# Softmax times V: the verdict is loaded in the last pass, and the first head's spread stands in the middle branch

## The chip, the cores and the metric

The kernel runs on one core of one Trainium2 chip. The metric is the device time of one execution in microseconds; the median of several runs is given. The core has five engines: TensorE (matmuls; "PE" and "PEld" in the profile, its sequencer "PEq"), VectorE ("DVE"), ScalarE ("ACT"), GpSimd ("POOL") and SyncE ("SP"), which here issues all transfers. Each engine runs its own instruction stream; they meet through semaphores.

## The reference

```python
# scores: (8, 12, 1024, 1024) float32, v: (8, 12, 1024, 64) float32, both drawn from a normal distribution
scores_max = np.max(scores, axis=-1, keepdims=True)
attn = np.exp(scores - scores_max)
attn = attn / (np.sum(attn, axis=-1, keepdims=True) + 1e-8)
return np.matmul(attn, v).astype(np.float32)
```

There are 96 heads. Scores are 403 MB, V and the output 25 MB each.

## The kernel before, in words

**Passes and heads.** A `For_i` loop makes `PASSES` = 24 passes, each over `AHEAD` = 4 heads. They are handled two at a time, so that a pass has `K` = 2 steps, k = 0 and k = 1 (the text calls such a step a head: the first head, the second head). A step has 128 partitions (64 for each of its two heads) and `R` = 16 rows of 1024 scores in each partition.

**A row.** ScalarE takes the exponential, two rows an instruction (L460; one row at a time for the last four of the second head); the maximum is not subtracted. TensorE transposes the result in eight 128 x 128 blocks into PSUM (L473), VectorE copies it to `pt` (L485, L481), and TensorE multiplies it with `vones`, V with a column of ones at its side (L172), so that the sum of the exponentials comes out as one more column. The products of a row follow its transposes by `LAG` = 3 rows: `finish` takes the oldest row from `pending`. TensorE's order is written out by hand (`in_line`).

**Normalisation.** Three rows share a PSUM bank (`psO`), so that 16 rows make six groups and the last group has one row. `normalise` takes the reciprocal of the sums into a column of `seen` (`invert`, L150), and then VectorE multiplies with it, once for each half of the partitions (L158), into `out_bufs`.

**V.** A pass's V is loaded as `v_sb` (`load_v`, L308). GpSimd spreads it into `vones` with eight casts for each head (`spread_v`, L320): for k = 0 behind the last products of the first head, for k = 1 at the pass's end. In the last pass there is no further V, but the spread for k = 0 is executed all the same. GpSimd also puts finished rows by in `done` (L202), which is stored in the next pass.

**Branches.** `load_first` stands behind the transposes of the first head's last row. If more passes follow, it loads V, stores the pass before and loads the next pass's first scores (a condition inside cuts the load in three for the last passes). Otherwise it stores what the two passes before left. `last` stands at the end of the pass: either spread, put by and load, or, in the last pass, `end` (three stores of the last rows, L237), `fold` and `judge`. All five engines execute every branch, also those in which they have nothing to do; an engine that has skipped instructions raises its semaphore by as many in the other arm (the balance).

**The verdict.** Sums of exponentials may overflow for other inputs, and V may be too large. `seen` keeps the reciprocals and the largest |V|; `fold` reduces them (L352, L353). `judge` makes one column `right` of two comparisons (L361, L364), TensorE counts it with a matmul against ones (L369), and VectorE writes the count (L373). Behind the loop each engine loads the count into a register (`nc.values_load`, L511) and branches (L515) over `general`, the slow kernel, which is not executed for these inputs.

**Order of transfers.** SP issues in program order; the names in `queued` chain the instructions. The loop does without a barrier between passes (`iteration_sync="reg_based"`): waits are on semaphore values that registers hold.

Of the kernel before, what the change touches and what calls it, by code (L numbers as in the profile page):

```python
# [9 lines left out]
FP16 = mybir.dt.float16  # L10
# [16 lines left out]
def kernel(  # L27
# [16 lines left out]
    G = 3  # L44
# [87 lines left out]
    def in_line(op):  # L132

        if line:
            after(op, line[-1])
        line.append(op)
# [16 lines left out]
    def normalise(k, st, g):  # L153
# [10 lines left out]
            fills.append(norm)  # L164
        norms[k] = norm

    def finish(u):

        _, k, r, pt, st = u
        g, i = r // G, r % G  # L170
        for c in range(C):
            product = nc.tensor.matmul(  # L172
                out=st["psO"][g][:, i * M : (i + 1) * M],
                lhsT=pt[:, c * P : (c + 1) * P],
                rhs=vones[:, k, c].rearrange("p t n -> p (t n)")[:, 0:M],
                start=(c == 0),
                stop=(c == C - 1),
            )
            in_line(product)
        if i == G - 1 or r == R - 1:  # L180
            normalise(k, st, g)
        if r == R - 1 and k < K - 1:
            fold()
            spread_v(k)

    def behind(a, b, reason):

# [63 lines left out]
    stores, fills, ends, norms = [], [], [], {}  # L251
    writers, users = {}, {}

    def apart(a, b, reason="stores of two heads are disjoint"):
# [19 lines left out]
    def load(k, m, parts=(R,), r=0, **cond):  # L274
        rows_n = sc_rows[bass.ds(m, 1), k].rearrange("o x r k -> (o x) r k")
        for rows in parts:
            queue(
                nc.sync.dma_start(  # L278
                    out=s_bufs[k][:, r : r + rows, :], in_=rows_n[:, r : r + rows, :], **cond
                )  # L280
            )
            r += rows

    def load_first(m):

# [30 lines left out]
    def spread_v(k, behind_rows=False):  # L316

        for t in range(T):
            for s in range(S):
                op = nc.gpsimd.tensor_copy(  # L320
                    out=vones[s * Q : (s + 1) * Q, k, :, t, 0:D].rearrange(
                        "i (h l) d -> i h l d", l=L
                    ),
                    in_=v_sb[(k * T + t) * Q : (k * T + t + 1) * Q, :, s],
                )
# [16 lines left out]
    def small(name, dtype=FP32):  # L342
        turn[name] = turn.get(name, 0) + 1
        return small_pool.tile([P, 1], dtype, name=f"{name}{turn[name]}")

    count = small_pool.tile([1, 1], I32, name="count")
    right = small("right", FP16)

    def fold():

        n = K * R + 1
        nc.vector.tensor_reduce(out=seen[:, 0:1], in_=seen[:, 0 : n + 1], axis=X, op=ALU.min)  # L352
        nc.vector.tensor_reduce(  # L353
            out=seen[:, n + 1 : n + 2], in_=seen[:, 1 : n + 2], axis=X, op=ALU.max
        )

    def judge(bank):

        n = K * R + 1
        part = small("part")  # L360
        nc.vector.tensor_scalar(  # L361
            out=part, in0=seen[:, n + 1 : n + 2], scalar1=1.0, scalar2=None, op0=ALU.is_le
        )
        nc.vector.scalar_tensor_tensor(  # L364
            out=right, in0=seen[:, 0:1], scalar=1.0 / SUM_MAX, in1=part, op0=ALU.is_ge, op1=ALU.mult
        )
        cell = bank[0:1, G * M : G * M + 1]
        in_line(
            nc.tensor.matmul(  # L369
                out=cell, lhsT=right[:], rhs=vones[:, 0, 0, 0, D : D + 1], start=True, stop=True  # L370
            )
        )
        nc.vector.tensor_copy(out=count[:], in_=cell)  # L373

    def general():

# [39 lines left out]
                out=o_rows[bass.ds(n, 1)].rearrange("o p d -> (o p) d"), in_=out_row  # L416
            )

    def last(m, bank):

        before = queued[-1:]
        k = K - 1
        with tc.If(m < PASSES - 1) as cmp:
            n = nc.snap(m + 1, min_val=1, max_val=PASSES - 1)
            with tc.If(m < PASSES - 2) as cmp3:
                behind(put_by(0), norms[0], "all rows are there")
                spread_v(k, True)
                watch_v()
                put_by(k)
            with cmp3.Else():  # L430
                spread = spread_v(k)
                watch = watch_v()
                gate = nc.gpsimd.tensor_copy(out=cell, in_=out_bufs[k][:, R - 1, D - 1 : D])
                for op in (watch, spread):
                    behind(gate, op, "the values have been read")
                put_spare()
            with tc.If(m < PASSES - 3) as cmp2:  # L437
# [12 lines left out]
    def heads(m):  # L450

        for k in range(K):
            st = dict(psO=[take(psO_bufs) for g in range(GROUPS)])
            for r in range(R):
# [29 lines left out]
                elif r % EB == EB - 1:  # L484
                    copy = nc.vector.tensor_copy(out=pt2[:], in_=psT2[:])  # L485
# [12 lines left out]

    assert BH % AHEAD == 0 and BH >= 3 * AHEAD and SK == Q * S * C and K == 2
    load_v(0)  # L500
# [5 lines left out]
    with tc.For_i(0, PASSES, 1, iteration_sync="reg_based") as m:  # L506
# [1 line left out]
        line.clear()  # L508
        heads(m)

    good = nc.values_load(  # L511
        count[:], min_val=0, max_val=P,
        skip_runtime_bounds_check_because="a count of partitions, which is compared and no address",
    )
    with tc.If(good < P, preferred_fallthrough_block=False):  # L515
        general()


# [28 lines left out]
```

## Time and profile before

| | |
|---|---|
| median of 3 runs | 1058.47 us (1058.43 to 1059.35) |
| the profiled execution | 1058.32 us, its span 1056.6 us |
| bytes moved | 453 MB, mean 429 GB/s |
| busy: TensorE, VectorE, ScalarE, GpSimd | 77%, 67%, 71%, 40% |

The page's times are microseconds from the start of the span. "L320" is line 320 of the kernel. In a line of the timeline stand the start, the length, the engine, the line and the operation, its output and input, the count, and in brackets how long the engine was idle before and what ended that. In an answer about one line stand the count, the shortest, median and longest duration in ns, and the first and last start. A window's line has its length, the busy time of TensorE, its weight loads, VectorE, ScalarE and GpSimd with their counts, then the granted TensorE clock, the transfer engines' share and GB/s.

### The profile page before, as it was taken

Reading aid. Unit: us, or ns where it says so; the run is one execution under the profiler, and the core shown is the slowest. Engines: PE = TensorE matmul, PEld = TensorE weight load, DVE = VectorE, ACT = ScalarE, POOL = GpSimd, SP = SyncE. Lnnn points to the kernel's source line nnn. Section 1 sums busy time; section 2 is a strip of 40 time slices with the busy share of each in tenths; the row PEclk is TensorE's granted clock in tenths of the full one; section 3 lists DMA queues with packets and bytes.
Section 4 is the critical chain, followed back from the end, with each engine's and each line's share of the span. In section 5 each row is a group of like instructions: output and inputs, shape, how many; then the busy total and the mean of one; then the engine's idle time right before and its main releaser. Section 6 shows DMA issues by size and latency. Waiting matters only on the chain.

```text
span 1056.6 us, 32648 instructions
## 1 busy us (share of the span) xinstructions
PE 812.9 (77%) x12289; PEld 777.5 (74%) x12289; DVE 705.7 (67%) x1352; ACT 750.2 (71%) x484; POOL 423.6 (40%) x579
## 2 busy tenths in 40 slices
PE   3488678787787868878678877787687876878887
PEld 3488668686787867878678777787677866868786
DVE  2377666676676756768567675676656766667787
ACT  4487578776787667876778667786687856877985
POOL 3063343533525335343362433633426334353341
PEclk9799889888898988889888898898988988989999
DMA  9999999999999999999999999999999999999997
GB/s 397 438 437 429 406 452 437 427 422 429 444 437 437 437 432 441 437 429 429 429 422 434 437 437 437 437 437 417 457 429 429 432 414 439 437 437 423 428 420 325
DMA packets 16692, 453.06 MB, mean 429 GB/s; under 512 B 1840, under 2 KB 1968, under 8 KB 2992
## 3 DMA queue, kind: packets, MB, share of 16 engines
q1 hardware_dynamic: 16688, 452.99, 99.6%
q8 instruction: 4, 0.07, 0.0%
HBM read 427.82 MB, written 27.26 MB: 431 GB/s over the span
## 4 chain that ended last, share of the span: by engine, by line
DMA 61%; PE 14%; ACT 10%; PEld 9%; DVE 3%; POOL 1%; issue 1%; SPq 0%; ACTq 0%; POOLq 0%; PEldq 0%; DVEq 0%
DMA s_nat<-in_scores_dram 61%; ACT p_nat L460 10%; PE psT L473 7%; PE psO L172 7%; PEld L172 4%; PEld L473 4%; DVE pt L485 3%; POOL vones L320 1%; POOL done L202 0%; SPq L278 0%; DVE out_sb L158 0%; DVE seen L150 0%; ACTq L460 0%; DVE pt L481 0%; SPq L308 0%
## 5 line engine op out<-in xcount | busy, mean ns | idle before, releaser
L460 ACT ACTIVATE p_nat<-s_nat 128x2048 f16<-128x2048 f32 (+1 forms) x432 | 702.5, 1709 | 284.2 <-SPq L437 157.9
L473 PE MATMUL psT<-ident,p_nat 128*128 128x128 f16 x6144 | 520.6, 235 | 212.7 <-ACT p_nat L460 212.5
L485 DVE COPY pt<-psT 128x2048 f16<-128x2048 f16 x336 | 411.3, 1224 | 307.2 <-PE L473 143.3
L473 PEld LDWEIGHTS <-p_nat 128*128 128x128 f16 x6144 | 435.6, 120 | 227.9 <-ACT p_nat L460 225.3
L172 PE MATMUL psO<-vones,pt 128*128 128x130 f16 x6144 | 498.4, 227 | 25.0 <-DVE pt L481 10.7
L320 POOL CAST vones<-v_sb 32x512 f16<-32x512 f32 x392 | 238.1, 607 | 619.0 <-PE L473 296.1
L172 PEld LDWEIGHTS <-pt 128*128 128x128 f16 x6144 | 400.0, 101 | 45.0 <-DVE pt L485 27.2
L158 DVE TENSOR_TENSOR out_sb<-psO,seen 64x192 f32<-64x192 f32 (+1 forms) x576 | 192.0, 333 | 24.4 <-POOL done L202 2.5
L202 POOL COPY done<-out_sb 32x1024 f32<-32x1024 f32 x176 | 182.5, 1037 | 10.4
L481 DVE COPY pt<-psT 128x1024 f16<-128x1024 f16 x96 | 63.3, 681 | 1.5
L150 DVE RECIPROCAL seen<-psO 128x3 f32<-128x3 f32 (+1 forms) x288 | 49.4, 172 | 11.7 <-PE L473 6.6
L334 ACT ACTIVATE p_nat<-v_sb 128x2048 f16<-128x2048 f32 x24 | 45.6, 1899 | 0.0
L441 ACT CAST ident<-ident 128x128 f16<-128x128 f32 x2 | 0.6, 298 | 6.9 <-PE psO L172 6.9
L334 ACT ACT_TABLE_LOAD x1 | 1.3, 1283 | 5.6 <-DMA v_sb<-in_v_dram 5.6
L352 DVE TENSOR_REDUCE seen<-seen 128x1 f32<-128x34 f32 x25 | 4.7, 189 | 0.8
L334 ACT ACTIVATION_READ_ACCUMULATOR p_nat<-v_sb 128x1 f32 x24 | 4.5, 188 | 0.0
L353 DVE TENSOR_REDUCE seen<-seen 128x1 f32<-128x34 f32 x25 | 4.5, 178 | 0.0
L108 DVE MEMSET done<- 128x1024 f32 x2 | 1.8, 912 | 1.2 <-DVEq L506 1.0
L214 POOL COPY v_sb<-out_sb 128x1024 f32<-128x1024 f32 x2 | 2.0, 1040 | 0.0
L369 PE MATMUL psO<-vones,right 128*1 128x1 f16 x1 | 0.2, 164 | 2.0 <-DVE right L364 2.0
L369 PEld LDWEIGHTS <-right 128*1 128x1 f16 x1 | 0.1, 79 | 2.2 <-DVE right L364 2.2
L364 DVE SCALAR_TENSOR_TENSOR right<-seen,part 128x1 f16<-128x1 f32 x1 | 0.5, 519 | 0.0
(13 smaller groups left out, 2.0 us busy)
## 6 DMA issues: line engine op xcount, KB each, us to landing
v_sb<-in_v_dram SPq DMA_DIRECT2D x24, 1024.0 KB, 14.0
out_dram<-done SPq DMA_DIRECT2D x24, 1024.0 KB, 8.6
s_nat<-in_scores_dram SPq DMA_DIRECT2D x4, 4096.0 KB, 18.7
s_nat<-in_scores_dram SPq DMA_DIRECT2D x8, 2048.0 KB, 25.9
s_nat<-in_scores_dram SPq DMA_DIRECT2D x6, 1024.0 KB, 29.0
s_nat<-in_scores_dram SPq DMA_DIRECT2D x4, 512.0 KB, 26.7
out_dram<-v_sb SPq DMA_DIRECT2D x1, 1024.0 KB
s_nat<-in_scores_dram SPq DMA_DIRECT2D x43, 28.7
```

Of the source, the lines that this page charges most:

```text
L150: nc.vector.reciprocal(out=recip, in_=psO[:, :, D : D + 1])
L158: norm = nc.vector.tensor_tensor(out=out_bufs[k][part, g * G : g * G + rows, :], in0=psO[part, :, t * N : t * N + D], in1=recip[part].to_b ...
L172: product = nc.tensor.matmul(out=st["psO"][g][:, i * M : (i + 1) * M], lhsT=pt[:, c * P : (c + 1) * P], rhs=vones[:, k, c].rearrange("p t ...
L202: put = nc.gpsimd.tensor_copy(out=done[to : to + J, a], in_=out_bufs[k][at : at + J].rearrange("x r d -> x (r d)"),)
L320: op = nc.gpsimd.tensor_copy(out=vones[s * Q : (s + 1) * Q, k, :, t, 0:D].rearrange("i (h l) d -> i h l d", l=L), in_=v_sb[(k * T + t) * Q ...
L334: return nc.scalar.activation(out=junk, in_=v_sb[:].rearrange("p h s l d -> p (h s l d)"), func=mybir.ActivationFunctionType.Abs, scale=1. ...
L352: nc.vector.tensor_reduce(out=seen[:, 0:1], in_=seen[:, 0 : n + 1], axis=X, op=ALU.min)
L353: nc.vector.tensor_reduce(out=seen[:, n + 1 : n + 2], in_=seen[:, 1 : n + 2], axis=X, op=ALU.max)
L460: exp = nc.scalar.activation(out=p_nat[:, g : g + rows, :].rearrange("p r (x v) -> p x r v", v=Q * L), in_=s_bufs[k][:, r + g : r + g + ro ...
L473: turned = nc.tensor.transpose(out=psT[:, c * P : (c + 1) * P], in_=p_row[:, c // L, c % L, :], identity=ident16[:],)
L481: copy = nc.vector.tensor_copy(out=pt, in_=psT)
L485: copy = nc.vector.tensor_copy(out=pt2[:], in_=psT2[:])
```

## The change

Four things. `load_first` is called in `finish`, behind the first head's last normalisation, and the first head's `spread_v` stands inside its branch, so that it is not executed in the last pass. The last row of the second head is normalised inside the branch of `last`: by VectorE as before in all passes but the last, where `normalise_last` lets ScalarE multiply. `judge` makes two columns and two matmuls that add up in one PSUM cell, in another bank; the count is of both comparisons, 256 where all is well. And every engine loads the count into the register `verdict` at the end of the last pass; behind the loop only the comparison is left.

```diff
+    def normalise_last(k, st, g):
+
+        assert R - g * G == 1
+        psO, recip = invert(k, st, g)
+        for t in range(T):
+            part = slice(t * W, (t + 1) * W)
+            norm = nc.scalar.mul(
+                out_bufs[k][part, g * G, :], psO[part, 0, t * N : t * N + D], recip[part, 0]
+            )
+            lasts.append(norm)
...
-        if i == G - 1 or r == R - 1:
+        if i == G - 1 or (r == R - 1 and k < K - 1):
             normalise(k, st, g)
         if r == R - 1 and k < K - 1:
+            load_first(u[0], k)
             fold()
-            spread_v(k)
...
-    def load_first(m):
+    def load_first(m, k):
...
             with cmp2.Else():
                 queued[:] = then
                 load(0, n, (8, 4, 4))
+            spread_v(k)
         with cmp.Else():
...
-    right = small("right", FP16)
+    right = small_pool.tile([P, 2], FP16, name="right")
+
+    nothing = nc.gpsimd.memset(small("mark"), 0.0)
...
     def judge(bank):
 
         n = K * R + 1
-        part = small("part")
-        nc.vector.tensor_scalar(
-            out=part, in0=seen[:, n + 1 : n + 2], scalar1=1.0, scalar2=None, op0=ALU.is_le
-        )
-        nc.vector.scalar_tensor_tensor(
-            out=right, in0=seen[:, 0:1], scalar=1.0 / SUM_MAX, in1=part, op0=ALU.is_ge, op1=ALU.mult
-        )
+        for j, at, limit, op in (
+            (0, 0, 1.0 / SUM_MAX, ALU.is_ge),
+            (1, n + 1, 1.0, ALU.is_le),
+        ):
+            nc.vector.tensor_scalar(
+                out=right[:, j : j + 1],
+                in0=seen[:, at : at + 1],
+                scalar1=limit,
+                scalar2=None,
+                op0=op,
+            )
         cell = bank[0:1, G * M : G * M + 1]
...
+        for j in range(2):
+            in_line(
+                nc.tensor.matmul(
+                    out=cell,
+                    lhsT=right[:, j : j + 1],
+                    rhs=vones[:, 0, 0, 0, D : D + 1],
+                    start=(j == 0),
+                    stop=(j == 1),
+                )
+            )
+        return nc.vector.tensor_copy(out=count[:], in_=cell)
+
+    verdict = nc.alloc_registers("verdict", engines=mybir.ALL_ENGINES)
+    nc.regs_mov(verdict, 0)
...
-    def last(m, bank):
+    def last(m, st):
...
         with tc.If(m < PASSES - 1) as cmp:
+            normalise(k, st, GROUPS - 1)
...
         with cmp.Else():
             queued[:] = before
+            normalise_last(k, st, GROUPS - 1)
             end()
             fold()
-            judge(bank)
+            counted = judge(st["psO"][-2])
+            for read in nc.regs_load(verdict, count[:]):
+                behind(read, nothing, "a wait that is known beforehand")
+                apart(counted, read, "there is one count")
...
-                if r == R - 1 and k < K - 1:
-                    load_first(m)
...
-        last(m, st["psO"][-1])
-        for store in ends:
+        last(m, st)
+        for op in ends + lasts:
             for fill in fills:
-                apart(fill, store, "no pass comes behind the last stores")
+                apart(fill, op, "no pass comes behind the last rows")
...
-    good = nc.values_load(
-        count[:], min_val=0, max_val=P,
-        skip_runtime_bounds_check_because="a count of partitions, which is compared and no address",
-    )
-    with tc.If(good < P, preferred_fallthrough_block=False):
+    good = nc.snap(verdict, donate=True, min_val=0, max_val=2 * P)
+    with tc.If(good < 2 * P, preferred_fallthrough_block=False):
         general()
```

More of the change, by code (lines that the diff above doesn't have):

```diff
@@ L249, in end @@
             )
-    stores, fills, ends, norms = [], [], [], {}
+    stores, fills, ends, lasts, norms = [], [], [], [], {}
     writers, users = {}, {}
@@ L359, in judge @@
         n = K * R + 1
-        part = small("part")
-        nc.vector.tensor_scalar(
-            out=part, in0=seen[:, n + 1 : n + 2], scalar1=1.0, scalar2=None, op0=ALU.is_le
-        )
-        nc.vector.scalar_tensor_tensor(
-            out=right, in0=seen[:, 0:1], scalar=1.0 / SUM_MAX, in1=part, op0=ALU.is_ge, op1=ALU.mult
-        )
-        cell = bank[0:1, G * M : G * M + 1]
-        in_line(
-            nc.tensor.matmul(
-                out=cell, lhsT=right[:], rhs=vones[:, 0, 0, 0, D : D + 1], start=True, stop=True
-            )
-        )
-        nc.vector.tensor_copy(out=count[:], in_=cell)
+        for j, at, limit, op in (
[9 more added lines that the diff above has]
+            )
+        cell = bank[0:1, G * M : G * M + 1]
+        for j in range(2):
[7 more added lines that the diff above has]
+                )
+            )
+        return nc.vector.tensor_copy(out=count[:], in_=cell)
+    verdict = nc.alloc_registers("verdict", engines=mybir.ALL_ENGINES)
+    nc.regs_mov(verdict, 0)
     def general():
@@ L509 @@
         heads(m)
-    good = nc.values_load(
-        count[:], min_val=0, max_val=P,
-        skip_runtime_bounds_check_because="a count of partitions, which is compared and no address",
-    )
-    with tc.If(good < P, preferred_fallthrough_block=False):
+    good = nc.snap(verdict, donate=True, min_val=0, max_val=2 * P)
+    with tc.If(good < 2 * P, preferred_fallthrough_block=False):
         general()
```

## The prediction

> **What bounds the kernel now.** I read the page first: span, chain, queues.
>
> ```profile
> span 1056.6 us, 32648 instructions
> DMA 61%; PE 14%; ACT 10%; PEld 9%; DVE 3%; POOL 1%; issue 1%; SPq 0%; ACTq 0%; POOLq 0%; PEldq 0%; DVEq 0%
> q8 instruction: 4, 0.07, 0.0%
> s_nat<-in_scores_dram SPq DMA_DIRECT2D x43, 28.7
> ```
>
> The chain lies for 61% in score loads. Such a load takes 28.7 us from issue to landing, and it carries 8.4 MB (128 x 16 x 1024 x 4 bytes). The windows by stage, one in the middle and the last one, show what the transfer engines did meanwhile.
>
> ```profile
> 500.00:544.00 44.00, 34.05 (x517) 32.47 (x514) 29.83 (x57) 31.15 (x20) 18.02 (x24) 0.88 0.99 429
> 1040.00:1057.00 17.00, 9.94 (x164) 9.19 (x161) 11.85 (x29) 6.26 (x6) 4.85 (x8) 0.88 0.66 262
> ```
>
> In the middle the DMA share is 0.99 at 429 GB/s. At that rate 8.4 MB need 19.6 us, so a load waits some 9 us in a full queue before its data move. A compute engine that is late by less than that in a middle pass therefore moves nothing: the middle passes are bound by bytes, and the change leaves the bytes alone. Next, the chain in order of time towards the end.
>
> ```profile
> 930.68 28.58 DMA s_nat<-in_scores_dram
> 959.36 1.92 ACT p_nat L460
> ...
> 1051.81 0.61 POOL vones L320
> ```
>
> Its last transfer lands at 959.36. From there compute sets the pace: the last two passes have no queue to hide in. Its last pieces are GpSimd's spread (L320), work whose output no later pass reads. So two places count: the last 8 us, and the seam between the heads in the last two passes. Here are the last 8 us in the timeline.
>
> ```profile
> 1048.48 5.27 POOL L320 CAST vones<-v_sb 32x512 f16<-32x512 f32 x8 [24.32 <-PE psT L473]
> 1050.70 0.17 DVE L150 RECIPROCAL seen<-psO 128x1 f32<-128x1 f32 x1
> 1050.90 0.47 DVE L158 TENSOR_TENSOR out_sb<-psO,seen 64x64 f32<-64x64 f32 x2
> 1051.41 0.19 DVE L352 TENSOR_REDUCE seen<-seen 128x1 f32<-128x34 f32 x1
> 1051.51 0.18 DVE L353 TENSOR_REDUCE seen<-seen 128x1 f32<-128x34 f32 x1
> 1051.72 0.15 DVE L361 TENSOR_SCALAR part<-seen 128x1 f32<-128x1 f32 x1
> 1051.91 0.52 DVE L364 SCALAR_TENSOR_TENSOR right<-seen,part 128x1 f16<-128x1 f32 x1
> 1052.48 0.16 PE L369 MATMUL psO<-vones,right 128*1 128x1 f16 x1 [2.00 <-DVE right L364]
> 1052.69 0.15 DVE L373 CAST count<-psO 1x1 int32<-1x1 f32 x1 [0.26 <-PE psO L369]
> ```
>
> GpSimd ends at 1048.48 + 5.27 = 1053.75, the count is written at 1052.84, the third store is issued when the pair of products ends at 1051.37. The answers on single lines and the waits of SP's queue, in windows behind 1051, give what follows.
>
> ```profile
> L237 SPq DMA_DIRECT2D out_dram<-out_sb x1: 332/332/332, 1051.4 to 1051.4; - x1
> out_dram<-out_sb SPq DMA_DIRECT2D x1, 128.0 KB, 2.0
> SPq L506 <- POOLq L423: 0.4, 1, 0.4
> SPq L506 <- DMA out_dram<-out_sb: 0.3, 1, 0.3
> L542 SPq DRAIN  x1: 7/7/7, 1053.9 to 1053.9; - x1
> L542 POOLq EVENT_SEMAPHORE  x1: 17/17/17, 1054.2 to 1054.2; - x1
> L542 DVEq EVENT_SEMAPHORE  x1: 21/21/21, 1054.6 to 1054.6; - x1
> L511 SPq TENSOR_LOAD <-count x1: 480/480/480, 1054.6 to 1054.6; - x1
> L511 DVEq TENSOR_LOAD <-count x1: 562/562/562, 1054.7 to 1054.7; - x1
> L515 DVEq COMPARE_BRANCH  x2: 57/59/61, 1055.3 to 1055.4; - x2
> ```
>
> The third store lands 2.0 us after its issue, at 1053.4. SP waits 0.3 us for it, then 0.4 us for GpSimd, and is through at 1053.9. GpSimd reaches the barrier behind the loop at 1054.2, everyone is let go at 1054.6, the five engines load the count (0.48 to 0.56), and VectorE branches at 1055.3. From there to 1056.6 runs an ending that the change does not touch.
>
> **The change, part by part.** *The spread in the last pass goes.* GpSimd skips 5.27 us and leaves the chain. Next late is SP: it still has the landing at 1053.4, then, with nothing to wait for, a few hundredths to its end.
>
> *ScalarE normalises the last row.* Two products move from VectorE (pair 0.47) to ScalarE. No row shows ScalarE multiplying a 64 x 64 tile out of PSUM by a column. Its exponentials bound it.
>
> ```profile
> L460 ACT ACTIVATE p_nat<-s_nat 128x2048 f16<-128x2048 f32 x336 | 611.1, 1899 | 283.5 <-SPq L437 157.9 <-DMA s_nat<-in_scores_dram 123.5 <-PE L473 1.1
> L460 ACT ACTIVATE p_nat<-s_nat 128x1024 f16<-128x1024 f32 x96 | 93.5, 1043 | 0.7 <-PE L473 0.3 <-PE L172 0.2 <-PE psO L172 0.2
> ```
>
> (1899 - 1043) / 1024 is 0.836 ns an element, with 187 ns fixed; 64 elements make 240 ns, the pair 0.48. A hand-over costs 0.05 (VectorE ends at 1052.43, TensorE starts at 1052.48). The reciprocal ends at 1050.87, so ScalarE works from 1050.92 to 1051.40 and the third store is issued at 1051.45 instead of 1051.4. I take +0.05. [...]
>
> *The verdict.* Without the products, VectorE's reductions start at 1050.91, 0.50 earlier. The first comparison runs from 1051.22 to 1051.37 (0.15, L361's duration), the second by 1051.52 where 0.52 stood. L364 had run until a GpSimd cast ended (1051.81 + 0.61 = 1052.42, the piece in the chain above), so part of its 0.52 was probably that. Two matmuls of 0.16 end at 1051.74; the copy ends at 1051.94, 0.90 earlier than before.
>
> *The register loads move into the last pass*, which is the added wait. Each engine waits for the count, then loads it. Behind that wait stand, on TensorE, VectorE, ScalarE and GpSimd, only the loop's end. On SP stand the branch's balancing semaphores and SP's waits for the last landing; the stores are ahead of it. SP's issue ends at 1051.45 + 0.33 = 1051.78, it waits till 1051.99 and has its register at 1052.47. Before, it was free at 1051.4 + 0.33 = 1051.73 and through at 1053.9, of which 0.3 + 0.4 were the two waits: 1.47 of its own. So 1052.47 + 1.47 = 1053.94. The landing at 1053.45 is covered by that, and SP becomes the last to arrive.
>
> *Behind the loop.* GpSimd took from 1054.2 to 1054.55 or so to let the others go. Now it waits for SP at 1053.94 + 0.05, and they go at 1054.35: 0.20 earlier. From there to VectorE's branch were 0.7; without the load some 0.15 are left: 0.55 earlier.
>
> *The middle branch stands later.* Every engine crosses it behind the first head's last normalisation instead of ahead of it. On SP no instruction lies between the old and the new place, so the value load, the store, the score load (in the last pass the two stores) keep their order; on GpSimd the spread is the first work of a pass either way. For VectorE the order at the seam is what can change. It stands so in the last pass:
>
> ```profile
> 1036.49 0.17 DVE L150 RECIPROCAL seen<-psO 128x1 f32<-128x1 f32 x1
> 1036.58 1.20 DVE L485 COPY pt<-psT 128x2048 f16<-128x2048 f16 x1
> 1037.81 0.48 DVE L158 TENSOR_TENSOR out_sb<-psO,seen 64x64 f32<-64x64 f32 x2
> 1038.32 0.19 DVE L352 TENSOR_REDUCE seen<-seen 128x1 f32<-128x34 f32 x1
> 1038.63 1.22 DVE L485 COPY pt<-psT 128x2048 f16<-128x2048 f16 x1
> ```
>
> The copy of the next rows now runs between the reciprocal and the products. If the branch is a fence, the products must come first and the copy starts some 0.55 later, with the same work done by 1038.6. TensorE may stall for up to 0.5 at that point, but the copy behind it starts when it did. I take 0; bounds -0.2 and +0.6 in each of two passes.
>
> *The last row's normalisation behind the branch, and the balance.* In all other passes VectorE normalises just inside the branch, and engines owe a semaphore for what they skipped.
>
> ```profile
> L423 DVEq COMPARE_BRANCH  x47: 75/97/125, 67.8 to 1050.9; - x47
> L423 DVEq ALU_OP  x23: 45/45/45, 68.9 to 1017.7; - x23
> L423 DVEq EVENT_SEMAPHORE  x23: 21/21/21, 69.0 to 1017.8; - x23
> ```
>
> A branch is 0.1, a balance 0.07. One more pair an engine and pass is covered by the 9 us of queue in the middle; it would cost 0.07 a pass (1.6 in all) if that cover were gone, and costs up to 0.1 in the last pass but one, which is inside the bounds above. The new memset and the register moves stand ahead of the loop, one small instruction an engine; I take them at 0.
>
> **Sum.** -0.20 at the barrier and -0.55 for the loads: -0.75. Against the profiled execution (1058.32, its span of 1056.6 and 1.72 around it) that is 1057.57; that execution lies 0.15 below the median of the runs, so I forecast 1058.47 - 0.75 = 1057.7. Should SP be held by the landing alone (through at 1053.6), it is -1.1; should SP's own work grow by 0.35, -0.4.
>
> **The rivals.** *SP is not delayed by its load.* If its register is there before its issue ends, the landing decides and the time is 1057.4. For it: the count comes 0.9 earlier. Against: the load follows the stores in the program.
>
> *The seam costs, and the kernel ends slower.* The branch fences VectorE's copy behind products and reductions in the last two passes, and TensorE, busy almost throughout, never gets the time back: up to 0.48 + 0.28 for each pass, with branches and balances 0.9, so 1.8 in both. With -0.75 that is +1.05: 1059.5. For it: no transfer is in the chain behind 959.36. Against: VectorE does the same work, and its next copy is not later. It decides once TensorE's stall at the seam exceeds some 0.4.
>
> *A toll in every pass.* [...] The trace bears little of it out: 4 instruction packets in the whole run, none per pass, and branches of about 0.1. A stall below 9 us would hide in the middle; one that delays the loads themselves by 0.15 to 0.25 a pass gives +3.5 to +5.8, less 0.75: 1061 to 1063.5.
>
> *The change does not do what it says*: the engines still wait at the end, or the barrier was held by something not shown. Then only the count's 0.9 moves, off the chain: 1058.4.
>
> **How the numbers follow.** Forecast 0.55; SP not delayed 0.15; seam 0.14; nothing 0.08; toll 0.05; a gain beyond 0.2% 0.03, from a seam that gets better in both passes. 0.2% is 2.1 us, about what a measurement of this kernel can tell from no change; faster means below 1056.4, slower above 1060.6. The seam at its dearest touches that bound with a slow median, so 0.03 of it goes to slower, and of the landing case 0.01 to faster. Faster 0.04, slower 0.08, same 0.88. The range takes the landing case with an early store (1057.0) and most of the seam (1059.3).
>
> **What would show it.** In the changed profile: no L320 cast behind 1040; GpSimd idle at the end; two ScalarE products of about 0.24 near 1050.9 and the third store within 0.1 of 1051.4; comparisons of 0.15 and two matmuls; loads of some 0.5 near 1052; the release behind the loop no later than 1054.4 against the same last matmul, and about 0.15 from there to the branch. Wrong would be: score loads of the middle passes that land later than 28.7 after their issue, or fewer than 429 GB/s there, a TensorE wait above 0.4 at the seam, a table load ahead of the products, or SP through later than 1054.

## The result, and the profile after

| | before | after |
|---|---|---|
| median | 1058.73 us (10 runs, 1058.37 to 1059.35) | 1061.11 us (10 runs, 1060.60 to 1062.67) |
| the profiled execution | 1058.32 us, span 1056.6 us | 1060.83 us, span 1059.0 us |
| last reciprocal (L150) starts | 1050.70 | 1053.51 |
| from there to the end of the span | 5.90 | 5.49 |

The changed kernel is slower: 1.0025 of the time before, interval 1.0016 to 1.0034. The forecast was 1057.7 in 1057.0 to 1059.3, so the result lies 1.8 us above its range. The last two lines of the table say where to look. The ending did get shorter, by 0.41 us. But the last reciprocal, which marks the end of the last pass's work, comes 2.81 us later. The loss is made ahead of everything that the change was costed on.

First the page of the changed kernel, its answer on the loads, one middle window and two pieces of its chain:

```profile
span 1059.0 us, 32978 instructions
q8 instruction: 4, 0.07, 0.0%
s_nat<-in_scores_dram SPq DMA_DIRECT2D x43, 28.7
...
500.00:544.00 44.00, 34.33 (x497) 33.24 (x498) 28.16 (x55) 31.25 (x20) 18.05 (x24) 0.84 0.99 429
...
930.77 28.58 DMA s_nat<-in_scores_dram
959.45 1.92 ACT p_nat L493
```

Loads still land 28.7 us after their issue, the middle window still moves 429 GB/s at a DMA share of 0.99, the instruction queue has its 4 packets, and the last scores land at 959.45 instead of 959.36. The middle passes are untouched. What is lost is lost behind 959.

The next view is ScalarE's timeline there. In the kernel before:

```profile
973.99 1.90 ACT L334 ACTIVATE p_nat<-v_sb 128x2048 f16<-128x2048 f32 x1
978.57 0.30 ACT L441 CAST ident<-ident 128x128 f16<-128x128 f32 x1 [2.59 <-PE psO L172]
979.38 29.14 ACT L460 ACTIVATE p_nat<-s_nat 128x2048 f16<-128x2048 f32 x18 [0.51 <-PE psO L172]
1008.42 1.90 ACT L334 ACTIVATE p_nat<-v_sb 128x2048 f16<-128x2048 f32 x1
1014.73 0.30 ACT L441 CAST ident<-ident 128x128 f16<-128x128 f32 x1 [4.32 <-PE psO L172]
1015.54 1.91 ACT L460 ACTIVATE p_nat<-s_nat 128x2048 f16<-128x2048 f32 x1 [0.51 <-PE psO L172]
```

And in the changed kernel:

```profile
978.73 0.30 ACT L470 CAST ident<-ident 128x128 f16<-128x128 f32 x1 [4.57 <-PE psO L183]
979.10 1.91 ACT L346 ACTIVATE p_nat<-v_sb 128x2048 f16<-128x2048 f32 x1
...
981.01 29.12 ACT L493 ACTIVATE p_nat<-s_nat 128x2048 f16<-128x2048 f32 x18
1015.50 0.30 ACT L470 CAST ident<-ident 128x128 f16<-128x128 f32 x1 [5.37 <-PE psO L183]
1016.05 1.91 ACT L346 ACTIVATE p_nat<-v_sb 128x2048 f16<-128x2048 f32 x1 [0.25 <-PE psO L183]
...
1017.96 1.89 ACT L493 ACTIVATE p_nat<-s_nat 128x2048 f16<-128x2048 f32 x1
```

Read the order of the lines. Before, ScalarE's look at V (`watch_v`, L334: an instruction of 1.9 us that finds the largest |V|) runs right behind the exponentials, at 973.99, while ScalarE would otherwise wait for TensorE's last products. After, the same instruction (L346) stands behind the copy of the identity (L470), which waits for those products. It has left idle time and stands between the passes. From the copy to the next pass's first exponential it was 0.81 us; now it is 2.28 and 2.46. The two instructions belong to two inner branches of `last`, "look and spread" and "load the next scores", and the compiled streams have them in the opposite order, although nobody moved them in the source. The only step of the change that touches this branch is the last row's normalisation, VectorE's at the head of this arm and ScalarE's in the arm of the last pass.

TensorE waits for that exponential. Its timeline at the starts of the two passes, before and then after (the bracket is its idle time):

```profile
981.47 1.06 PE L473 MATMUL psT<-ident,p_nat 128*128 128x128 f16 x16 [1.22 <-ACT p_nat L460]
1017.55 1.06 PE L473 MATMUL psT<-ident,p_nat 128*128 128x128 f16 x16 [1.12 <-ACT p_nat L460]
```

```profile
982.96 3.42 PE L506 MATMUL psT<-ident,p_nat 128*128 128x128 f16 x32 [2.55 <-ACT p_nat L493]
1019.91 2.31 PE L506 MATMUL psT<-ident,p_nat 128*128 128x128 f16 x19 [2.72 <-ACT p_nat L493]
```

Its gaps doubled, to 2.55 and 2.72. And something else shows in the windows of 3 us behind these gaps (the third number from the right is the granted clock); before, then after:

```profile
982.00:985.00 3.00, 2.12 (x35) 1.79 (x33) 1.89 (x2) 3.00 (x3) 2.76 (x5) 1.00 1.01 431
1019.00:1022.00 3.00, 2.44 (x40) 2.27 (x41) 2.16 (x2) 3.00 (x3) 2.65 (x5) 1.00 1.02 437
```

```profile
982.00:985.00 3.00, 2.04 (x19) 1.87 (x20) 0.11 (x1) 3.00 (x3) 2.73 (x5) 0.59 1.02 437
1019.00:1022.00 3.00, 2.09 (x19) 1.83 (x20) 0.26 (x1) 3.00 (x3) 2.76 (x5) 0.68 0.99 426
```

Before, TensorE works at full clock; after, it does 19 matmuls in windows where it did 35 and 40, only in part because it starts later. Cut into windows of 0.5 us, the granted clock there is 0.50 for 3.4 us, then 1.00 again. As an estimate from these two numbers, such a spell takes up to 3.4 x 0.5 = 1.7 us of TensorE's work, where TensorE has work for all of it. So there are two suspects with one origin: ScalarE's 1.9 us itself, and the spells behind the longer gap.

Last, the ending of the changed kernel, timeline first, then answers on single lines:

```profile
1053.51 0.17 DVE L150 RECIPROCAL seen<-psO 128x1 f32<-128x1 f32 x1
1053.77 0.64 ACT L173 ACTIVATE out_sb<-psO,seen 64x64 f32<-64x64 f32 x2 [6.50 <-DVE seen L150]
1053.93 0.26 DVE L379 TENSOR_SCALAR right<-seen 128x1 f16<-128x1 f32 x2
1054.15 0.26 PE L389 MATMUL psO<-vones,right 128*1 128x1 f16 x2 [0.85 <-DVE right L379]
1054.44 0.34 SPq L248 DMA_DIRECT2D out_dram<-out_sb  x1
1054.45 0.15 DVE L397 CAST count<-psO 1x1 int32<-1x1 f32 x1 [0.26 <-PE psO L389]
...
L479 ACTq TENSOR_LOAD <-count x1: 477/477/477, 1054.7 to 1054.7; - x1
L479 SPq TENSOR_LOAD <-count x1: 678/678/678, 1055.0 to 1055.0; - x1
L570 SPq DRAIN  x4: 7/7/7, 1057.2 to 1058.6; - x4
L570 DVEq EVENT_SEMAPHORE  x3: 21/21/21, 1057.7 to 1058.9; - x3
L543 DVEq COMPARE_BRANCH  x2: 57/59/61, 1057.8 to 1057.9; - x2
```

GpSimd's spread is gone: its last L332 cast starts at 1022.1. SP is the last to arrive, through at 1057.2; everyone is let go at 1057.7 and VectorE branches 0.1 later, where it took 0.7 before.

### The profile page after: what moved, and what is told of

Its sections match the earlier page's. It is cut to its first block, busy times and chain, and to the rows that moved or that the text cites. A ratio compares the mean times of both kernels' runs of the same rounds, so it can differ in the third digit from the quotient of the medians.

```text
span 1059.0 us, 32978 instructions
## 1 busy us (share of the span) xinstructions
PE 816.0 (77%) x12290; PEld 780.8 (74%) x12290; DVE 704.2 (67%) x1350; ACT 752.7 (71%) x486; POOL 419.8 (40%) x572
## 5 line engine op out<-in xcount | busy, mean ns | idle before, releaser
L332 POOL CAST vones<-v_sb 32x512 f16<-32x512 f32 x384 | 234.0, 609 | 594.2 <-PE L506 309.1
L158 DVE TENSOR_TENSOR out_sb<-psO,seen 64x192 f32<-64x192 f32 x574 | 191.5, 334 | 43.8 <-issue 16.1
L346 ACT ACTIVATE p_nat<-v_sb 128x2048 f16<-128x2048 f32 x24 | 46.0, 1915 | 15.2 <-PE L183 5.6
L150 DVE RECIPROCAL seen<-psO 128x3 f32<-128x3 f32 (+1 forms) x288 | 49.5, 172 | 8.3 <-PE L506 6.7
L470 ACT CAST ident<-ident 128x128 f16<-128x128 f32 x2 | 0.6, 298 | 9.9 <-PE psO L183 9.9
L346 ACT ACTIVATION_READ_ACCUMULATOR p_nat<-v_sb 128x1 f32 x24 | 4.5, 188 | 0.0
## 6 DMA issues: line engine op xcount, KB each, us to landing
s_nat<-in_scores_dram SPq DMA_DIRECT2D x43, 28.7
```

The source lines that it names most:

```text
L150: nc.vector.reciprocal(out=recip, in_=psO[:, :, D : D + 1])
L158: norm = nc.vector.tensor_tensor(out=out_bufs[k][part, g * G : g * G + rows, :], in0=psO[part, :, t * N : t * N + D], in1=recip[part].to_b ...
L332: op = nc.gpsimd.tensor_copy(out=vones[s * Q : (s + 1) * Q, k, :, t, 0:D].rearrange("i (h l) d -> i h l d", l=L), in_=v_sb[(k * T + t) * Q ...
L346: return nc.scalar.activation(out=junk, in_=v_sb[:].rearrange("p h s l d -> p (h s l d)"), func=mybir.ActivationFunctionType.Abs, scale=1. ...
```

## The experiments

Each kernel ran 11 times or, where a count stands, fewer, beside the kernel before on the same chip (medians there 1058.65 to 1058.87). Behind each median stand the ratio to the kernel before and its 95% interval; the ratio is estimated from the runs of both and is not the quotient of the medians. The theories: **A**, the order of ScalarE's two inner branches; **B**, the middle branch, which now stands between VectorE's two products of group 4 and makes it wait there; **C**, a toll in every pass, already out by the unchanged middle; **D**, TensorE's half clock behind its gaps.

### The order of the inner branches

**e1_order**, the changed kernel with ScalarE's order put back:

```diff
-                watch_v()
+                watch1 = watch_v()
...
-                nc.scalar.copy(out=ident16[:], in_=ident32[:])
+                again = nc.scalar.copy(out=ident16[:], in_=ident32[:])
+                after(again, watch1)
+                after(again, watch)
```

> The changed kernel, with an order edge that puts ScalarE's look at V (the instruction that reads v_sb, 1.9 us) ahead of the copy of the identity in the branch at the pass's end, as it stood in the kernel before. Theory A (the order of the two inner branches): the changed kernel loses because ScalarE looks at V only behind the wait for TensorE's last transposes, which puts 1.9 us between two passes where compute sets the pace; then the time falls from 1061.1 to between 1058.6 and 1059.1, and the last pass's first exponential starts within 0.3 of 1015.5. Theory B (VectorE's stall of 0.62 at the middle branch): nothing moves, 1060.7 to 1061.3. Theory C (a toll in every pass): nothing moves either, and the middle passes are longer than before.

Measured: 1059.64 us (1057.87 to 1060.34), 1.0004 of before (0.9995 to 1.0013). Some 1.5 of the 2.4 us are gone. That is the way theory A said, but 0.5 us above its band. ScalarE's order is that of before:

```profile
974.44 1.90 ACT L346 ACTIVATE p_nat<-v_sb 128x2048 f16<-128x2048 f32 x1
...
979.18 0.30 ACT L470 CAST ident<-ident 128x128 f16<-128x128 f32 x1 [2.74 <-PE psO L183]
980.08 29.14 ACT L495 ACTIVATE p_nat<-s_nat 128x2048 f16<-128x2048 f32 x18 [0.60 <-PE psO L183]
```

The first exponential stands 0.90 behind the copy again. TensorE's gaps are 1.33 and 1.28, and its profile still has a half-clock spell behind each.

**e2_swap**, the kernel before with the load's branch written ahead of the look's in the source:

```diff
+            with tc.If(m < PASSES - 3) as cmp2:
+                ...
             with tc.If(m < PASSES - 2) as cmp3:
...
-            with tc.If(m < PASSES - 3) as cmp2:
-                ...
```

> The kernel before, with nothing of the change, only the two inner branches at the pass's end written in the other order, so that the identity is copied ahead of the look at V. Theory A: this alone costs what the changed kernel lost by it, 2.0 to 2.6: 1060.7 to 1061.3. Theories B and C: 1058.5 to 1059.0, no change.

Measured: 1058.90 us (1058.38 to 1060.18), ratio 1.0000 (0.9991 to 1.0009). It tests nothing of theory A: in its trace the look at V (974.21) still stands ahead of the copy (977.65). The compiler had ordered the branches its own way. What the miss does show is that the order in the source does not decide the order in the stream.

**s2_forced**, the same with the order forced by edges:

```diff
+                again = nc.scalar.copy(out=ident16[:], in_=ident32[:])
...
-                watch_v()
+                after(watch_v(), again)
...
+                after(watch, again)
```

> The kernel before, with one thing changed: order edges put ScalarE's copy of the identity (the branch with the load of the next head) ahead of its look at V (the branch for the late passes), as the changed kernel has them. Theory A (the order of these two branches costs the time: the 1.9 us look at V stands between the last pass's matmuls and its first exponential): the last pass's first exponential starts about 2.4 us later than in the kernel before (near 1018.0), and the time is 1060.2 to 1061.2, with no other part of the change in it. Theory B (the middle branch between VectorE's two products is the cause): 1058.7, as before. Theory D (TensorE's half-clock spells at the starts of the passes are the cause, and the gap begets them): TensorE's gap at the pass starts grows from 1.2 to 2.5 us, and spells of granted clock 0.50 stand there; if no spell follows the gap, 1060.2 at most.

Measured: 1061.68 us (1060.27 to 1062.06), 1.0026 (1.0017 to 1.0035), the sign of theory A, 0.5 us above its band. Its timelines of ScalarE and of TensorE:

```profile
1015.04 0.30 ACT L429 CAST ident<-ident 128x128 f16<-128x128 f32 x1 [4.80 <-PE psO L172]
1015.60 1.91 ACT L334 ACTIVATE p_nat<-v_sb 128x2048 f16<-128x2048 f32 x1 [0.26 <-PE psO L172]
...
1017.51 18.13 ACT L461 ACTIVATE p_nat<-s_nat 128x2048 f16<-128x2048 f32 x10
...
983.06 3.70 PE L474 MATMUL psT<-ident,p_nat 128*128 128x128 f16 x32 [2.55 <-ACT p_nat L461]
1019.46 1.08 PE L474 MATMUL psT<-ident,p_nat 128*128 128x128 f16 x16 [2.72 <-ACT p_nat L461]
```

This kernel has nothing of the change but the order of two branches, and it loses as much as the whole change, with the same gaps of 2.55 and 2.72. The order is sufficient for the loss: that is shown, and by e1_order most of the loss goes with it.

### Which part turns the order round

**e3_middle**, before with the middle branch and the spread moved, nothing else:

```diff
         if r == R - 1 and k < K - 1:
+            load_first(u[0], k)
             fold()
-            spread_v(k)
...
+            spread_v(k)
...
-                if r == R - 1 and k < K - 1:
-                    load_first(m)
```

> The kernel before with the middle branch alone: loads and the first head's spread behind the last normalisation, and no spread in the last pass. Theory A: the spread's end gives 0.2 to 0.4, VectorE's stall at the branch takes 0.3 to 0.5, so 1058.6 to 1059.0. Theory B: the stall costs 2 or more, 1060.5 to 1061. Theory C: 1060.5 to 1061.5, with middle passes longer.

Measured: 1059.35 us (1058.09 to 1060.73), 1.0002 (0.9993 to 1.0012), between the bands of theories A and B. The look at V stands at 973.93, in the idle time, so this part of the change leaves the order alone.

**e5_vector**, the changed kernel with the last row left to VectorE, outside the branch, as before:

```diff
-        if i == G - 1 or (r == R - 1 and k < K - 1):
+        if i == G - 1 or r == R - 1:
...
-            normalise(k, st, GROUPS - 1)
...
-            normalise_last(k, st, GROUPS - 1)
```

> The changed kernel, with the last row normalised by VectorE ahead of the branch in every pass, as before; middle branch, two comparisons and register loads as in the change. The inner branches then stand in their old order. Theory A: 1058.4 to 1059.0, and a tail from the last product to the end 0.3 to 0.5 shorter than before. Theories B and C: 1060.5 to 1061.3.

Measured: 1059.56 us (1058.59 to 1060.08), 1.0003 (0.9994 to 1.0013). It differs from the changed kernel in these three lines, and its ScalarE has the look at V back in the idle time:

```profile
974.36 1.90 ACT L346 ACTIVATE p_nat<-v_sb 128x2048 f16<-128x2048 f32 x1
```

So **the last row's normalisation inside the branch is what turned the order round**. The median lies 0.6 us above theory A's band again. Both arms of the branch lose their call here, so whether VectorE's call in the one or ScalarE's in the other does it was not told apart. Why the compiler orders so was not tested either; that the spread, which shares its block with the look at V, stands near the normalisation in that branch is only a guess.

**e4_verdict**, before with two comparisons, two matmuls and the register loads in the last pass. The expectation speaks of ScalarE normalising the last row; the kernel that ran left that row with VectorE, outside the branch:

> The kernel before, with the verdict's part of the change alone: two comparisons summed by two matmuls, and every engine loads the count in the last pass; the last row is ScalarE's there, but VectorE normalises it in all other passes inside the outer branch, so the order of the inner branches may swap as in the changed kernel. Middle branch and spread are those of before. Theory A: if the look at V stands behind the identity's copy, 1060.2 to 1061.2, and if it stands ahead of it, 1058.2 to 1058.9. Theory B: the middle branch isn't moved, so 1058.2 to 1058.9 in either order. In both GpSimd's spread (5.3 us) is back at the end, so the tail from the last reciprocal to the end is 5.6 to 5.9, not below.

Measured: 1058.55 us (1058.10 to 1059.69), 0.9999 (0.9990 to 1.0008). The look at V stands at 974.28. The verdict's part alone shortens the ending of its profiled execution by 0.26 (5.64 us from the last reciprocal to the end, with GpSimd's spread still there), and the medians can't tell it from nothing. It adds little to what the spread's removal gives by itself: e3_middle and m2_branch, which load the count behind the loop, have endings of 5.27 and 5.47.

### The middle branch

In the changed kernel VectorE's timeline at the first head's end shows theory B's suspect, a wait of 0.62 us between the two products:

```profile
1001.82 0.35 DVE L158 TENSOR_TENSOR out_sb<-psO,seen 64x192 f32<-64x192 f32 x1
1002.79 0.36 DVE L158 TENSOR_TENSOR out_sb<-psO,seen 64x192 f32<-64x192 f32 x1 [0.62 <-issue]
```

**m2_branch**, e3_middle with the branch placed behind VectorE's 1.2 us copy:

```diff
-            load_first(u[0], k)
...
+                if ahead is not None and t + s == 0:
+                    after(op, ahead)
...
+                    if k > 0 and r == LAG:
+                        load_first(m, k - 1, copy)
```

> The kernel of e3_middle (before, with the spread moved into the middle branch), with the middle branch placed behind VectorE's 1.2 us copy of the next rows, so that it no longer stands between the two products of group 4. Theory B: VectorE's wait of 0.62 us at that place goes, and with it what e3_middle stands above before: 1058.0 to 1058.6. Theory A: the order of the inner branches is that of before here as well as in e3_middle, so it moves by no more than 0.3 against e3_middle: 1059.0 to 1059.6. Theory D: the time goes with the number of half-clock spells behind 955, whichever way the branch stands.

Measured: 1059.41 us (1057.79 to 1061.38), 1.0010 (1.0001 to 1.0019). No gain, against theory B. But look at the runs: six lie between 1057.79 and 1059.41, five between 1060.90 and 1061.38, none between. The profiled ones of m2_branch (1057.79) and of e3_middle (1060.42) fall on the two sides. Behind 955, m2_branch has one half-clock spell of 3.4 us; e3_middle has 6.8 us at 960 and 3.4 us at 994, and its last reciprocal comes 2.80 later. In this pair of traces the time goes with the spells, not with the branch; the spells of the other runs aren't on record.

**y1_branch**, the changed kernel with the same move of the branch and the order left wrong; **v4_both**, the same move with e1_order's edges:

> The changed kernel with the middle branch placed behind VectorE's copy alone; the look at V stays behind the identity's copy, as in the changed kernel. With e1_order (the other repair alone, 1059.64) and v4_both (both, 1058.42) it completes the square. Theory A: the order is the price, so 1060.6 to 1061.5, within 0.5 of the changed kernel. Theory B (the middle branch costs as much as the order): about 1059.9, 1.2 below the changed kernel, which is what the step from e1_order to v4_both was.

> The changed kernel with both repairs: the look at V ahead of the identity's copy, and the middle branch behind VectorE's copy. Theory A alone: as e1_order, 1059.6. Theories A and B together: the seam is that of before and the shorter tail (0.4) is left, 1058.0 to 1058.6, a little faster than before. Theory D: 1059.6 or more wherever the profile shows two or more half-clock spells behind 955, and below 1058.7 where it shows one.

Measured: y1_branch 1060.96 us (10 runs, 1060.30 to 1062.10), 1.0021 (1.0012 to 1.0031); v4_both 1058.42 us (1058.01 to 1059.35), 0.9998 (0.9989 to 1.0007). With the order wrong, the branch's place is worth 0.15 us, which the intervals can't tell from nothing; in the pair from e3_middle to m2_branch it is worth nothing; only from e1_order to v4_both did 1.2 us go by the medians, and there the intervals overlap. That pair is also one with two spells behind the pass starts against none. Theory B has no price of its own that these runs could show. v4_both is the fastest of the variants that contain the whole change; it beats the changed kernel, and the kernel before can't be told from it.

### TensorE's clock

**x1_filled**, s2_forced with 32 matmuls of 114 columns, which nobody reads, in TensorE's gap at the head of each pass; and **x3_short**, the same with 8 matmuls of 456 columns:

```diff
+                if k == 0 and r == 0:
+                    some = vones[:, 0, 0:4].rearrange("p c t n -> p (c t n)")
+                    for _ in range(8):
+                        in_line(
+                            nc.tensor.matmul(
+                                out=st["psO"][0][:, 0:456], lhsT=some[:, 0:P],
+                                rhs=some[:, 0:456], start=True, stop=True,
+                            )
+                        )
```

> The kernel of s2_forced (before, with the two inner branches in the changed kernel's order) with 32 matmuls of 114 columns put at the head of each pass on TensorE; nobody reads what they write. They fill some 2 us of TensorE's gap between the passes and leave ScalarE's order alone. If the time lost comes from the 1.9 us look at V standing ahead of the exponentials (theory A), the first exponential of the last pass stays near 1017.5 and the time 1061.2 to 1061.9. If it comes from TensorE's clock, which falls to 0.50 for 3.4 us behind the longer gap (theory D), the spells near 983 and 1020 go, each worth up to 1.7 us, and the time is 1058.5 to 1060.2. If the dummies themselves get in the way of the first transposes, it is slower than 1061.9.

> As x1_filled (the kernel of s2_forced with work that nobody reads in TensorE's gap at the head of each pass), with 8 matmuls of 456 columns in place of 32 of 114: the same 1.7 us or so of work in 16 instructions instead of 64. In x1_filled TensorE's last branch took 3.73 us, where it takes 0.33 in the kernel without the filler, and the instruction queue shows 5 packets instead of 4. If the length of TensorE's program did that, the branch is back at 0.33 and the tail behind the last reciprocal at 5.3 instead of 8.6. The last reciprocal stands near 1052.2, 1.4 ahead of s2_forced, if the filler takes away the two spells of half clock at the starts of the passes (theory D's share), and so the time is 1059.6 to 1060.6; what is left above before, 1.0 to 1.9, is the price of ScalarE's order (theory A's share). If the spells stay, 1061.3 to 1062.

Measured: x1_filled 1062.38 us (7 runs, 1061.02 to 1063.15), 1.0032 (1.0021 to 1.0043); x3_short 1059.30 us (1058.34 to 1060.23), 1.0005 (0.9996 to 1.0014), a little below what was expected. x3_short first: its ScalarE, its TensorE and its windows.

```profile
1015.17 1.91 ACT L334 ACTIVATE p_nat<-v_sb 128x2048 f16<-128x2048 f32 x1 [0.26 <-PE psO L172]
1017.08 27.23 ACT L461 ACTIVATE p_nat<-s_nat 128x2048 f16<-128x2048 f32 x16
...
1017.43 1.70 PE L477 MATMUL psO<-vones 128*128 128x456 f16 x8 [1.13 <-DVE out_sb L158]
1019.03 1.08 PE L486 MATMUL psT<-ident,p_nat 128*128 128x128 f16 x16
...
982.00:985.00 3.00, 2.42 (x28) 1.71 (x27) 0.74 (x1) 3.00 (x3) 2.70 (x6) 1.00 1.02 437
1019.00:1022.00 3.00, 2.28 (x38) 2.10 (x38) 1.22 (x1) 3.00 (x2) 2.63 (x6) 1.00 0.98 421
```

ScalarE has the wrong order still, and its look at V stands in the way as in s2_forced. TensorE does useless work in the gap, and with that its clock stays at 1.00 where it was 0.72 and 0.81 in the same windows of s2_forced. The last reciprocal moves from 1053.61 to 1052.24, and the median from 1061.68 to 1059.30. By the medians 2.4 of the 3.0 us that the order costs there go with the clock, and about 0.65 are left for the order itself. The profiled executions share it out otherwise: the last reciprocals come 2.91 (s2_forced) and 1.54 (x3_short) later than before's, so there 1.37 go with the clock; of the 1.54 a shorter tail gives 0.64 back. The profiled execution of s2_forced (1060.67) is one of its faster ones. No run put the filler into the kernel before, which has half-clock spells of its own, so either split is an estimate.

x1_filled kept the clock as well (its last reciprocal stands at 1052.17) and lost the time again at the very end. TensorE's last branch, in x1_filled and then in x3_short, with the instruction queue of x1_filled ahead of it:

```profile
q8 instruction: 5, 0.08, 0.0%
L527 PEldq COMPARE_BRANCH  x2: 74/1902/3729, 1056.1 to 1056.3; - x2
```

```profile
L528 PEldq COMPARE_BRANCH  x2: 74/200/327, 1056.2 to 1056.3; - x2
```

With 48 instructions more on TensorE, one branch waits 3.73 us instead of 0.33, together with a fifth instruction packet; with the shorter filler both are gone.

**x2_filled**, v4_both with 14 such matmuls of 114 columns:

> The kernel of v4_both (the changed kernel with both repairs) with 14 matmuls of 114 columns, which nobody reads, at the head of each pass. Where TensorE's spells of half clock cause the scatter between runs (theory D), the runs lie closer together and the median comes down by 0 to 0.5, to 1057.9 to 1058.4; if the spells come from elsewhere, nothing changes: 1058.2 to 1058.7.

Measured: 1058.60 us (1058.11 to 1059.47), 0.9998 (0.9989 to 1.0007). Nothing changes; its profile even has a spell at 982, behind a gap of 1.32 us ahead of the filler.

The traces in one table: TensorE's gaps at the starts of the last two passes, and whether a half-clock spell follows within 3 us (read off windows of 0.5 us).

| kernel | gaps, us | spells |
|---|---|---|
| before, e3_middle, m2_branch | 1.08 to 1.22 | 0 of 6 |
| e1_order, e5_vector, v4_both | 1.23 to 1.38 | 2 of 6 (both in e1_order) |
| e2_swap | 1.22 and 2.04 | 1 of 2 (behind 2.04) |
| e4_verdict | 1.33 and 2.02 | 2 of 2 |
| changed, s2_forced, y1_branch | 2.55 and 2.72 | 6 of 6 |
| x1_filled, x3_short (1.09 to 1.24 ahead of the filler) | - | 0 of 4 |
| x2_filled (1.23 and 1.32 ahead of the filler) | - | 1 of 2 |

What makes the gaps of 2.02 and 2.04 stays open: in e2_swap and e4_verdict the look at V stands in the idle time.

Most traces have a spell near 961 too, which this table leaves out. The next one counts all spells from 955 to the last reciprocal, one of 6.8 us as two, and gives the start of the last reciprocal, one execution for each kernel.

| spells | look at V ahead of the copy | look at V behind the copy |
|---|---|---|
| 1 | 1050.53 to 1051.14 (before, e2_swap, m2_branch, v4_both) | 1052.17 and 1052.24 (x1_filled, x3_short) |
| 2 | 1051.25 to 1052.64 (x2_filled, e4_verdict, e5_vector) | - |
| 3 or 4 | 1052.93 and 1053.33 (e1_order, e3_middle) | 1053.51 to 1053.61 (changed, s2_forced, y1_branch) |

At one spell the order costs 1.0 to 1.7 us (the kernels behind the copy hold the filler). With the changed order two or three more spells cost 1.3 to 1.4.

## Why the prediction was wrong

**The step that failed** is "the last row's normalisation behind the branch, and the balance", which it priced at a branch of 0.1 and a balance of 0.07, covered or "inside the bounds". It counted the instructions that the edit adds to a path. It didn't ask what the edit does to the order of what stands beside it. It had checked the order for SP and GpSimd, and for VectorE at the seam; ScalarE at the pass's end, where two independent branches stand in a row, it never looked at. That ScalarE works there, and that its 1.9 us were hidden only by their place, was to be read in the timeline of before. What it cost is 2.81 us in the profiled pair. By the profiled executions of s2_forced and x3_short, whose last reciprocals come 2.91 and 1.54 later than before's, about half of that is ScalarE's order itself and half is TensorE's clock; by their medians the clock has the larger share, 2.4 of 3.0.

**The rivals.** "The seam costs, and the kernel ends slower" had the sign, and a figure (1059.5) still 1.6 too low, but the wrong place: the branch does fence VectorE as it feared (0.62 us between the two products in the pass shown), and y1_branch finds 0.15 for that, no more than its noise. The place was the pass's end, not the seam between the heads, and the engine ScalarE. "A toll in every pass" fell with the unchanged 28.7 us and 4 packets. None of the changed kernel's branches takes more than 0.24 us; the one long branch that the runs showed, 3.73 us, is x1_filled's last, behind the loop. "Does not do what it says" is out: spread, loads and products all moved as described.

**What held.** The cover of the middle passes held in every number. The loads' removal was priced at 0.55 behind the release: from the release to the end of the span it was 2.0 and is 1.3. SP is the last to arrive, as the sum said.

**The sizes of the tail.** Of the 0.75 forecast, 0.41 came. From the end of the last reciprocal, the sum had the count written at +1.07 and it came at +0.92. (The sum gave the two matmuls 0.17 together, though each was to take 0.16; they took 0.26. The two comparisons, 0.26 and not 0.30 and nearer to the reductions, made up for it.) But the store goes out at +0.76 instead of +0.58, since ScalarE's pair takes 0.64 and not 0.48: 310 ns each, not the 240 that its exponentials gave. The early store that the low end of the range took is shown by no run: in the changed kernel's profile the store goes out 0.18 later behind the last reciprocal than the sum had it. And SP's issue of that store ends at 1054.78, behind the count (1054.60), where the sum had it end first. So SP's register load starts at 1055.0, 0.3 behind the other engines', and it takes 0.68 instead of 0.48. SP's own work behind it, from 1055.7 to 1057.2, is the 1.5 reckoned. So everyone was let go 4.2 us behind the last reciprocal, against 3.9 before and 3.7 forecast. The ending of before is also shorter where the last pass is late: s2_forced, which has the old ending whole, shows 5.29 instead of 5.90, since its spread ends 1.17 behind the last reciprocal there and 3.05 behind it in the kernel before. That is even less than the changed kernel's 5.49, so beside a pass as late as its own the new ending shows no gain.

## What to carry to other kernels

An edit inside a branch can reorder what the compiler places there; before costing such an edit, list for every engine the independent blocks that follow, and ask what each would cost on the other side of the wait that it hides under. Compare the compiled streams of both kernels, engine by engine, ahead of any sum, and pin an order that matters with an edge, as e1_order did. In a stage bound by TensorE, a longer gap can cost more than its length: here gaps that were 1.3 and 1.6 us longer were each followed by 3.4 us at a granted clock of 0.50. Price such a spell as well.

## What the runs showed of the hardware

**The clock can fall behind short gaps.** Behind 955, spells of granted clock 0.50 last 3.4 us (the changed kernel at 982.5) or 6.8 (y1_branch at 982). At the starts of the last two passes they follow gaps of TensorE of 2.0 us and more in 8 of 8 places, gaps of 1.23 to 1.38 us in 3 of 7, and gaps up to 1.22 in none of 7 (kernels without a filler). Elsewhere the gap's length does not decide. e4_verdict works on at a granted clock of 1.00 behind 3.16 us:

```profile
961.62 0.64 PE L503 MATMUL psT<-ident,p_nat 128*128 128x128 f16 x8 [3.16 <-ACT p_nat L490]
```

So does e2_swap behind 3.38 at 961.54, and x3_short behind 2.26 at 941.97. A gap of 1.91 at 993 is followed by a spell in e3_middle, and the same gap at 992 by none in m2_branch. Why e1_order's gaps of 1.33 and 1.28 beget spells and v4_both's 1.38 and 1.23 don't stays open.

**A longer program can make a branch wait.** 64 more instructions in TensorE's loop (32 matmuls and their weight loads) moved its last branch from 0.33 to 3.73 us; 16 more left it at 0.33, and no length between these tells where the step is.
